# Seven block products in place of eight, in three of the eight k-tile pairs of the gate and up matmuls of a transformer block

## The chip, the cores and the metric

One Trainium2 chip, one of its cores. A core has TensorE (PE in the profile), VectorE (DVE), ScalarE (ACT), GpSimd (POOL) and SyncE (SP, which issues the transfers here). The metric is the time of one execution on the device in microseconds (us); less is better.

## The reference

One layer of an encoder on 256 tokens of width 2048, all in float32:

```
xn = rms_norm(h, norm1_g); proj = xn @ w_in               # 2048 x 5120
att = differential attention (4 heads);  u = conformer convolution (1024 channels)
h  = h + concat(att, u) @ w_out                           # 2048 x 2048
hn = rms_norm(h, norm2_g)
a  = hn @ w_gate                                          # 2048 x 5632
bu = hn @ w_up                                            # 2048 x 5632
h  = h + (silu(a) * bu) @ w_down                          # 5632 x 2048
```

The change concerns the last four lines.

## The kernel before

**The split into two parts.** Every float32 factor is written as hi + lo, both of type float32r: hi is the rounded value (ScalarE, `act.copy`), lo the rest (VectorE, a subtraction). A product is then three matmuls: activation hi by weight hi (L306), activation lo by weight hi (L307), activation hi by weight lo (L312). The activation is the stationary operand (128 x 128), the weight the moving one (128 x 512).

**Chunks and blocks.** A block is 512 columns of a weight for all 256 tokens, that is two PSUM banks (tokens in two halves of 128, index m), summed over k-tiles of 128 rows. A block's k-tiles come in chunks of two: one transfer of 512 KB into `raw` (L270), one cast into `whi` (L275), one subtraction into `wlo` (L276), and 12 matmuls: the eight with the weight's hi first, then the four with its lo.

**The order.** All queues are written out by hand; nothing is reordered. `run_chunks` walks the list of chunks; when TensorE's part of chunk t is written out, the loads and splits of chunk t+2 (AHEAD = 2) have just been written. `raw` has five buffers, `whi` and `wlo` four each (RAW_BUFS, HL_BUFS), so that the split of a chunk waits until TensorE is done with the chunk four before it. Each engine takes its instructions strictly in this order. Beside the chunks run generators, resumed in the middle and at the end of each chunk: they write the norms, the attention, the convolution and the evictions, so that what they write stands in the engines' queues between two splits.

**The feed-forward part.** There are 11 blocks of 512 hidden columns. Each is a gate block of 16 k-tiles, whose result ScalarE turns into `sil` (L713), and an up block of 16 k-tiles, whose result VectorE multiplies with it (L721); then 16 transposes in TensorE (L729) and a hi/lo split (L732, L733) give the stationary tiles `ahi`, `alo` for w_down. After six blocks, and again after the other five (FGROUPS), w_down's products of these blocks are summed and added into `h` (L746). The factor 1/rms of the second norm, `rstd2`, is applied at the eviction (L713, L721).

**PSUM.** The eight banks are two pools: `acc` (four, the sums of blocks) and `aux` (four: transposes and the rest).

Of the kernel before, what the change touches and what calls it, by code (L numbers as in the profile page):

```python
# [28 lines left out]
W = 31  # L29
# [9 lines left out]
# where the rows of the gains and biases begin, 128 values to a row  # L39
# [41 lines left out]
def tile_block(  # L81
# [9 lines left out]
    lhs = ctx.enter_context(tc.tile_pool(name="lhs", bufs=KD))  # L91
# [7 lines left out]
    # ---------------------------------------------------------------- inputs and constants  # L99
# [7 lines left out]
    # the tensor engine's clock rises while the first loads are under way  # L107
# [9 lines left out]
    # a first use of the activation table before anything waits for it  # L117
# [11 lines left out]
    cw = const.tile([P, NCT, W], F32, tag="cw", name="cw")  # L129
# [15 lines left out]
    def late_constants():  # L145
# [10 lines left out]
        # q is scaled by 1/sqrt(d) through its gain  # L156
        act.mul(gb[:, 0, :], gb[:, 0, :], 1.0 / math.sqrt(DH))
        hd = DH // 2
        for i, key in enumerate("qk"):
            for m in range(NM):  # L160
                t = const.tile([P, 2, DH], F32, tag=f"gcs{key}{m}", name=f"gcs{key}{m}")
# [12 lines left out]
    def negative_lambda():  # L174
        """-lambda = exp(l2) - exp(l1) - lambda_init"""
# [5 lines left out]
    def rsqrt_mean(dst, ss, n, eps):  # L181
        """dst = (ss / n + eps) ** -0.5 on a few columns."""
# [4 lines left out]

    def lhs_pair(pfx, k):
        hi = lhs.tile([P, S], F32R, tag="lhi", name=f"{pfx}hi{k}")
        lo = lhs.tile([P, S], F32R, tag="llo", name=f"{pfx}lo{k}")  # L190
        return hi, lo

    def split_scaled(pair, src, scale):
        """hi + lo = src * scale, src in PSUM."""
# [21 lines left out]
    # banks of the aux pool that are read in a later stage than they are written  # L216
# [7 lines left out]
    # work of the vector engine that fills what the stream leaves free  # L224
# [12 lines left out]
    def side_step():  # L237
        """One step of the two oldest chains by turns: a step waits for the one before it."""
# [11 lines left out]
    def block(w, cols, ks, xs, done=None, bkey=None, first=True, last=True, spare=False, cuts=()):  # L250
        """Products of the k-tiles ks with columns of w, summed in two banks."""
# [6 lines left out]
        while i < len(ks):  # L258
# [4 lines left out]
                               done=done if i == len(ks) else None, spare=spare))  # L263

    def split_chunk(w, k0, nk, cols, width, **_):
        view = lambda t: t.rearrange("p (k n) -> p k n", n=width)[:, :nk]
        raw = view(wp.tile([P, NK * N], F32, tag="raw", name="raw", bufs=RAW_BUFS))
        o = 0
        for c, n in cols:
            sp.dma_start(out=raw[:, :, o : o + n],  # L270
# [539 lines left out]
```

## Time and profile before

| what | value |
|---|---|
| median of three runs | 1091.2 us (1090.16 to 1091.35) |
| profiled execution: span from the first to the last instruction | 1089.8 us |
| TensorE busy | 1079.0 us (99%) |
| weight loads of TensorE | 894.0 us (82%) |
| VectorE busy | 647.1 us (59%) |
| ScalarE busy | 509.6 us (47%) |
| moved by DMA | 203 MB, mean 186 GB/s |

The page gives only the span of the profiled execution; the median of the runs lies 1.4 us above it, which is what lies around the first and last instruction. Busy time of TensorE counts overlapping matmuls as they lie, so that a busy TensorE says only that it hardly waits; how fast it goes is read from the distance between the starts of neighbouring matmuls in the timeline. A wait costs time only if TensorE takes part in it.

### The profile page before, as it was taken

The page shows a single profiled execution, that of the slowest core. Times are in us where ns is not written, and L with a number is a line of the kernel's source. Part 1 is how long each engine was busy: PE and PEld are TensorE (multiplying, and loading weights), DVE is VectorE, ACT ScalarE, POOL GpSimd, SP SyncE. Part 2 cuts the span into 40 slices and gives each one's busy share as a digit, 9 for nine tenths or more (in the row PEclk, how much of TensorE's full clock was granted, in tenths as well). Part 3 has the DMA queues.
Part 4 walks back from the last instruction along what each step waited for, and adds up shares of the span by engine and source line. Part 5 has one row for each costly group of instructions (what it writes and reads, how often), then busy time and mean ns, then how long its engine had stood idle before and what let it go on. Part 6 is the DMA issues. An engine that isn't in the chain of part 4 may idle for free.

```text
span 1089.8 us, 13224 instructions
## 1 busy us (share of the span) xinstructions
PE 1079.0 (99%) x4952; PEld 894.0 (82%) x4952; DVE 647.1 (59%) x828; ACT 509.6 (47%) x719; POOL 49.1 (5%) x77
## 2 busy tenths in 40 slices
PE   8999999999999999999999999999999999999998
PEld 7988888877888888888888888888888888888886
DVE  4799989898766544544545454444454454544443
ACT  6644566755754544434444343333443444433332
POOL 0030112210100100000000000000000000000000
PEclk9999999999999999999999999999999999999999
DMA  8756665554456557666575555556666656653654
GB/s 241 233 177 198 190 189 161 154 169 155 155 181 206 174 172 220 187 192 189 168 214 184 192 192 193 192 187 190 194 186 192 189 169 211 186 192 108 219 204 146
DMA packets 118733, 203.02 MB, mean 186 GB/s; under 512 B 6932, under 2 KB 28878, under 8 KB 118668
## 3 DMA queue, kind: packets, MB, share of 16 engines
q1 hardware_dynamic: 118608, 202.14, 59.7%
q8 instruction: 39, 0.64, 0.2%
q14 instruction: 26, 0.21, 0.1%
q10 hardware_dynamic: 60, 0.03, 0.0%
HBM read 200.04 MB, written 2.10 MB: 185 GB/s over the span
## 4 chain that ended last, share of the span: by engine, by line
PE 92%; DVE 3%; ACT 2%; POOL 1%; issue 1%; DMA 1%; SPq 1%; DVEq 0%; ACTq 0%
PE acc L307 30%; PE acc L312 30%; PE acc L306 30%; DVE y L431 1%; DVE wlo L276 1%; PE ps_a L729 1%; ACT whi L275 1%; DMA h<-in_x_dram 1%; PE ps_o L643 1%; ACT junk L355 0%; POOL rsq L185 0%; PE ps_h L686 0%; SPq L360 0%; POOL fq L186 0%; SPq L270 0%
## 5 line engine op out<-in xcount | busy, mean ns | idle before, releaser
L276 DVE TENSOR_TENSOR wlo<-raw,whi 128x1024 fp32r<-128x1024 f32 (+1 forms) x377 | 456.4, 1221 | 337.3 <-ACT whi L275 304.5
L275 ACT CAST whi<-raw 128x1024 fp32r<-128x1024 f32 (+1 forms) x377 | 390.8, 1051 | 366.4 <-PE acc L307 326.6
L306 PE MATMUL acc<-whi,hhi 128*128 128x512 f32 x704 | 274.8, 390 | 0.0
L307 PE MATMUL acc<-whi,hlo 128*128 128x512 f32 x704 | 274.1, 389 | 0.0
L312 PE MATMUL acc<-wlo,hhi 128*128 128x512 f32 x704 | 189.2, 391 | 0.0
L307 PEld LDWEIGHTS acc<-whi,hlo 128*128 128x128 f32 x704 | 132.2, 188 | 27.3
L306 PEld LDWEIGHTS acc<-whi,hhi 128*128 128x128 f32 x704 | 132.2, 188 | 27.2
L312 PEld LDWEIGHTS acc<-wlo,hhi 128*128 128x128 f32 x704 | 131.4, 188 | 26.8
L306 PE MATMUL acc<-whi,ahi 128*128 128x512 f32 x384 | 150.7, 392 | 0.0
L307 PE MATMUL acc<-whi,alo 128*128 128x512 f32 x384 | 150.5, 392 | 0.0
L306 PE MATMUL acc<-whi,xhi 128*128 128x512 f32 (+1 forms) x352 | 130.0, 376 | 2.8 <-ACT xhi L196 2.8
L307 PE MATMUL acc<-whi,xlo 128*128 128x512 f32 (+1 forms) x352 | 128.6, 372 | 0.5 <-DVE xlo L197 0.4
L431 DVE SCALAR_TENSOR_TENSOR y<-upad,cw,y 128x256 f32<-128x256 f32 x240 | 103.6, 481 | 3.5 <-ACT y L424 3.0
L312 PE MATMUL acc<-wlo,ahi 128*128 128x512 f32 x384 | 103.6, 391 | 0.0
L312 PE MATMUL acc<-wlo,xhi 128*128 128x512 f32 (+1 forms) x352 | 88.7, 377 | 1.4 <-DVE wlo L276 1.2
L306 PEld LDWEIGHTS acc<-whi,ahi 128*128 128x128 f32 x384 | 72.1, 188 | 15.9
L307 PEld LDWEIGHTS acc<-whi,alo 128*128 128x128 f32 x384 | 72.1, 188 | 15.3
L312 PEld LDWEIGHTS acc<-wlo,ahi 128*128 128x128 f32 x384 | 71.9, 188 | 15.6
L306 PEld LDWEIGHTS acc<-whi,xhi 128*128 128x128 f32 x352 | 66.5, 189 | 14.7 <-ACT xhi L196 3.2
L307 PEld LDWEIGHTS acc<-whi,xlo 128*128 128x128 f32 x352 | 66.6, 189 | 11.9 <-DVE xlo L197 0.9
L312 PEld LDWEIGHTS acc<-wlo,xhi 128*128 128x128 f32 x352 | 62.3, 190 | 13.0 <-DVE wlo L276 2.2
L733 DVE TENSOR_TENSOR alo<-ps_a,ahi 128x512 fp32r<-128x512 f32 x22 | 15.2, 691 | 46.0 <-ACT ahi L732 46.0
(138 smaller groups left out, 544.2 us busy)
## 6 DMA issues: line engine op xcount, KB each, us to landing
raw<-in_w_gate_dram SPq DMA_DIRECT2D x88, 512.0 KB, 4.4
raw<-in_w_up_dram SPq DMA_DIRECT2D x88, 512.0 KB, 4.5
raw<-in_w_down_dram SPq DMA_DIRECT2D x88, 512.0 KB, 4.2
raw<-in_w_in_dram SPq DMA_DIRECT2D x48, 512.0 KB, 3.7
raw<-in_w_out_dram SPq DMA_DIRECT2D x32, 512.0 KB, 3.7
raw<-in_w_in_dram SPq DMA_DIRECT2D x62, 256.0 KB, 3.6
h<-in_x_dram SPq DMA_DIRECT2D x6, 256.0 KB, 6.1
out_dram<-h SPq DMA_DIRECT2D x6, 256.0 KB, 2.5
```

The source lines that it names most:

```text
L275: act.copy(hi, raw)
L276: dve.tensor_tensor(lo, raw, hi.bitcast(F32), ALU.subtract)
L306: pe.matmul(ps[m], xhi[:, ms], hi[:, j, :], start=c["first"] and j == 0, stop=False)
L307: pe.matmul(ps[m], xlo[:, ms], hi[:, j, :], start=False, stop=False)
L312: pe.matmul(ps[m], xhi[:, ms], lo[:, j, :], start=False, stop=c["last"] and j == nk - 1)
L431: dve.scalar_tensor_tensor(y[:, ct, :], src, wk, y[:, ct, :], ALU.mult, ALU.add)
L643: pe.matmul(o[:, m, :], wT[:, (0 if m == 0 else 1 + k), :], v_sb[k][:, hd * E : (hd + 1) * E], start=k == 0, stop=k == m)
L729: pe.transpose(pt[:, i, m * P : (m + 1) * P], aa[m][:, c : c + P], ident)
L733: dve.tensor_tensor(lo, pt, hi.bitcast(F32), ALU.subtract)
```

## The change

Block 0 of the feed-forward part stays as it was. In blocks 1 to 10 gate and up are computed together, as one product of a 2 x 2 arrangement: the rows are the two token halves, the inner index is a pair of k-tiles (k and k+8), the columns are up and gate. For three of the eight pairs (k = 0, 1, 2; NS = 3) this 2 x 2 product is formed with seven block products by Strassen's scheme in Winograd's form, from sums and differences of the activations (made once, in `make_forms`) and of the weight tiles (made for each pair, in `round_pair`). The other ten k-tiles are multiplied as before, in five chunks for gate and five for up. The seven products are summed in seven PSUM banks (the eighth is QX) over the three pairs, and the plain chunks are summed into those banks that each output needs last (Q2, Q4 for gate; Q3, QX for up). ORDER gives the 13 units of a block: s is a pair, g and u are plain chunks. `products_done` and `block_done` combine the banks into the four outputs. `make_forms` also multiplies the activations with `rstd2`, so that the evictions of these blocks need no scale.

Beside this: `whi` and `wlo` have three buffers instead of four and `raw` four instead of five; in the new blocks the cast runs three units ahead and the subtraction two; w_down is passed three times (after 4, 4 and 3 blocks) instead of twice; the stationary tiles for w_down share the pool of those of x and h, in tiles of two; some constants move to another pool; a pass of `transposed` is spread over more resumptions.

```diff
-RAW_BUFS = 5
+RAW_BUFS = 4
-HL_BUFS = 4
+HL_BUFS = 3
-FGROUPS = (6, 5)
+FGROUPS = (4, 4, 3)
+HK = KD // 2
+NS = 3
+REST = [k for k in range(KD) if k % HK >= NS]
+TWOS = [tuple(REST[i : i + 2]) for i in range(0, len(REST), 2)]
+BY_DMA = []
+ORDER = "sgggsggusuuuu"
+Q1, Q6, Q7, Q5, Q2, Q4, Q3, QX = range(8)
+PRODUCTS = ((Q1, 0, 5), (Q6, 5, 1), (Q7, 6, 2), (Q5, 4, 3), (Q2, 1, 6), (Q4, 3, 0), (Q3, 2, 4))
+HI_AHEAD, LO_AHEAD = 3, 2
...
     def run_chunks():
-        ready = deque()
         n = len(chunks)
-        i = 0
+        i = j = 0
         for t in range(n):
-            while i < min(n, t + 1 + lead(t)):
+            hi_lead, lo_lead = lead(t)
+            while i < min(n, t + 1 + hi_lead):
                 if i in before:
                     before[i]()
-                ready.append(split_chunk(**chunks[i]))
+                chunks[i]["load"](chunks[i])
+                chunks[i]["round"](chunks[i])
                 i += 1
-            multiply(chunks[t], *ready.popleft())
+                if hi_lead == lo_lead:
+                    chunks[j]["split"](chunks[j])
+                    j += 1
+            while j < min(n, t + 1 + lo_lead):
+                chunks[j]["split"](chunks[j])
+                j += 1
+            chunks[t]["multiply"](chunks[t])
...
@@ transposed: (was the end of up_done)
-            hi = fp.tile([P, 2, S], F32R, tag="ahi", name="ahi", bufs=FGROUPS[0] * 2)
-            lo = fp.tile([P, 2, S], F32R, tag="alo", name="alo", bufs=FGROUPS[0] * 2)
+            hi, lo = lhs_two("a", j * (N // P) + 2 * t)
             act.copy(hi, pt)
+            yield
             dve.tensor_tensor(lo, pt, hi.bitcast(F32), ALU.subtract)
...
             yield
+            yield
...
+    forms = {}
+    def make_forms():
+        fp = ffn["pool"]
+        ones = fp.tile([P, P], F32, tag="sum0", name="ones")
+        pool.memset(ones, 1.0)
+        diag = fp.tile([P, S], F32, tag="sum1", name="diag")
+        for m in range(NM):
+            act.activation(diag[:, m * P : (m + 1) * P], ident, AF.Copy, scale=rstd2[m])
+        yield
+        yield
+        ps = aux_ps.tile([P, N], F32, tag="aux", name="ps_r")
+        for m in range(NM):
+            pe.matmul(ps[:, m * P : (m + 1) * P], ones, diag[:, m * P : (m + 1) * P], start=True, stop=True)
+        yield
+        rb = fp.tile([P, S], F32, tag="sum2", name="rb")
+        act.copy(rb, ps[:, :S])
+        yield
+        hn = [fp.tile([P, HK, S], F32, tag="wt", name="hn"), fp.tile([P, HK, S], F32, tag="wb", name="hn", bufs=2)]
+        for k in range(KD):
+            while k not in hT:
+                yield
+            t = hn[k // HK][:, k % HK, :]
+            hi, lo = hT[k]
+            dve.tensor_tensor(t, hi.bitcast(F32), lo.bitcast(F32), ALU.add)
+            dve.tensor_tensor(t, t, rb, ALU.mult)
+            if k % 4 == 3:
+                yield
+        a11, a21 = (hn[0][:, :NS, m * P : (m + 1) * P] for m in range(NM))
+        a12, a22 = (hn[1][:, :NS, m * P : (m + 1) * P] for m in range(NM))
+        fhi = fp.tile([P, 7, NS, P], F32R, tag="fhi", name="fhi")
+        flo = fp.tile([P, 7, NS, P], F32R, tag="flo", name="flo")
+        f = fp.tile([P, 7, NS, P], F32, tag="wh", name="sums", bufs=2)
+        dve.scalar_tensor_tensor(f[:, 4], a21, -1.0, a22, ALU.mult, ALU.subtract)
+        dve.scalar_tensor_tensor(f[:, 5], f[:, 4], -1.0, a11, ALU.mult, ALU.subtract)
+        dve.tensor_tensor(f[:, 6], a11, a21, ALU.subtract)
+        dve.tensor_tensor(f[:, 2], a12, f[:, 5], ALU.subtract)
+        act.copy(fhi[:, 0], a11)
+        act.copy(fhi[:, 1], a12)
+        act.activation(fhi[:, 3], a22, AF.Copy, scale=-1.0)
+        yield
+        for i in (4, 5, 6, 2):
+            act.copy(fhi[:, i], f[:, i])
+        for i, a in ((0, a11), (1, a12)):
+            dve.tensor_tensor(flo[:, i], a, fhi[:, i].bitcast(F32), ALU.subtract)
+        dve.scalar_tensor_tensor(flo[:, 3], a22, -1.0, fhi[:, 3].bitcast(F32), ALU.mult, ALU.subtract)
+        yield
+        for i in (4, 5, 6, 2):
+            dve.tensor_tensor(flo[:, i], f[:, i], fhi[:, i].bitcast(F32), ALU.subtract)
+        yield
+        nr = HK - NS
+        chi = fp.tile([P, 2 * nr, S], F32R, tag="chi", name="chi")
+        clo = fp.tile([P, 2 * nr, S], F32R, tag="clo", name="clo")
+        for i in range(2):
+            act.copy(chi[:, i * nr : (i + 1) * nr], hn[i][:, NS:])
+        yield
+        for i in range(2):
+            dve.tensor_tensor(clo[:, i * nr : (i + 1) * nr], hn[i][:, NS:],
+                              chi[:, i * nr : (i + 1) * nr].bitcast(F32), ALU.subtract)
+        plain = {k: (chi[:, i, :], clo[:, i, :]) for i, k in enumerate(REST)}
+        forms.update(hi=fhi, lo=flo, plain=plain)
+    def load_pair(c):
+        c["b"] = ffn["pool"].tile([P, 4, N], F32, tag="wb", name="wb", bufs=2)
+        for i, w in enumerate((w_up, w_gate)):
+            sp.dma_start(out=c["b"][:, 2 * i : 2 * i + 2, :],
+                         in_=w.rearrange("(k p) n -> p k n", p=P)[:, c["k"] :: HK, c["col"] : c["col"] + N])
+    def round_pair(c):
+        fp = ffn["pool"]
+        assert "hi" in forms
+        b = c["b"]
+        c["t"] = t = fp.tile([P, 4, N], F32, tag="wt", name="wt")
+        c["hi"] = fp.tile([P, 7, N], F32R, tag="wh", name="wh", bufs=2)
+        dve.tensor_tensor(t[:, 2:4], b[:, 1:3], b[:, 0:1].to_broadcast([P, 2, N]), ALU.subtract)
+        dve.tensor_tensor(t[:, 1], b[:, 1], t[:, 3], ALU.add)
+        dve.tensor_tensor(t[:, 0], t[:, 1], b[:, 3], ALU.subtract)
+        act.copy(c["hi"][:, 4:], b[:, 1:])
+        act.copy(c["hi"][:, :4], t)
+    def split_pair(c):
+        c["lo"] = ffn["pool"].tile([P, 7, N], F32R, tag="wl", name="wl", bufs=2)
+        dve.tensor_tensor(c["lo"][:, 4:], c["b"][:, 1:], c["hi"][:, 4:].bitcast(F32), ALU.subtract)
+        dve.tensor_tensor(c["lo"][:, :4], c["t"], c["hi"][:, :4].bitcast(F32), ALU.subtract)
+    def sum_bank(c, i):
+        sums = c["sums"]
+        if i not in sums:
+            tag, pool_ = ("acc", acc_ps) if i < 4 else ("aux", aux_ps)
+            sums[i] = pool_.tile([P, N], F32, tag=tag, name=f"q{i}")
+        return sums[i]
+    def multiply_pair(c):
+        while "hi" not in forms:
+            resume()
+        fhi, flo, p = forms["hi"], forms["lo"], c["k"]
+        for n, (q, f, w) in enumerate(PRODUCTS):
+            ps = sum_bank(c, q)
+            first, last = c["first"].get(q), c["last"].get(q)
+            pe.matmul(ps, fhi[:, f, p, :], c["hi"][:, w], start=bool(first), stop=False)
+            pe.matmul(ps, flo[:, f, p, :], c["hi"][:, w], start=False, stop=False)
+            pe.matmul(ps, fhi[:, f, p, :], c["lo"][:, w], start=False, stop=bool(last))
+            if n in (1, 3, 5):
+                resume()
+        resume()
+        if c["done"]:
+            start(c["done"](c["sums"]))
+    def multiply_two(c):
+        hi, lo = c["hi"], c["lo"]
+        qs = (Q3, QX) if c["kind"] == "u" else (Q2, Q4)
+        for i, k in enumerate(c["ks"]):
+            x1, x2 = forms["plain"][k]
+            for m, q in enumerate(qs):
+                ms = slice(m * P, (m + 1) * P)
+                ps = sum_bank(c, q)
+                pe.matmul(ps, x1[:, ms], hi[:, i, :], start=i == 0 and bool(c["first"].get(q)), stop=False)
+                pe.matmul(ps, x2[:, ms], hi[:, i, :], start=False, stop=False)
+        resume()
+        for m, q in enumerate(qs):
+            ms = slice(m * P, (m + 1) * P)
+            for i, k in enumerate(c["ks"]):
+                pe.matmul(sum_bank(c, q), forms["plain"][k][0][:, ms], lo[:, i, :], start=False,
+                          stop=i == 1 and bool(c["last"].get(q)))
+        resume()
+        if c["done"]:
+            start(c["done"](c["sums"]))
+    def fast_block(j):
+        units, sums = [], {}
+        left = dict(s=list(range(NS)), g=list(TWOS), u=list(TWOS))
+        for kind in ORDER:
+            what = left[kind].pop(0)
+            c = dict(kind=kind, sums=sums, done=None, first={}, last={})
+            if kind == "s":
+                c.update(k=what, col=j * N, load=load_pair, round=round_pair, split=split_pair,
+                         multiply=multiply_pair, uses=[q for q, _, _ in PRODUCTS])
+            else:
+                c.update(ks=what, w=w_gate if kind == "g" else w_up, nk=2, width=N, cols=[(j * N, N)],
+                         rows=slice(what[0], what[1] + 1, what[1] - what[0]), by_dma=what in BY_DMA,
+                         load=load_chunk, round=round_chunk, split=split_chunk, multiply=multiply_two,
+                         uses=(Q3, QX) if kind == "u" else (Q2, Q4))
+            units.append(c)
+        assert not any(left.values())
+        for q in range(8):
+            users = [c for c in units if q in c["uses"]]
+            users[0]["first"][q] = users[-1]["last"][q] = True
+        [c for c in units if c["kind"] == "s"][-1]["done"] = products_done
+        units[-1]["done"] = lambda sums: block_done(j, sums)
+        chunks.extend(units)
+    halfway = {}
+    def products_done(q):
+        fp = ffn["pool"]
+        w1, u2, u3, w4 = (fp.tile([P, N], F32, tag=f"sum{i}", name=f"sum{i}") for i in range(4))
+        act.copy(w1, q[Q1])
+        yield
+        yield
+        dve.tensor_tensor(u2, q[Q6], w1, ALU.add)
+        dve.tensor_tensor(u3, q[Q7], u2, ALU.add)
+        dve.tensor_tensor(w4, q[Q5], u3, ALU.add)
+        dve.tensor_tensor(u2, q[Q5], u2, ALU.add)
+        yield
+        dve.tensor_tensor(w1, q[Q2], w1, ALU.add)
+        dve.tensor_tensor(u3, q[Q4], u3, ALU.add)
+        act.activation(w1, w1, AF.Silu)
+        act.activation(u3, u3, AF.Silu)
+        halfway.update(g=(w1, u3), u=(u2, w4))
+    def block_done(j, q):
+        while "g" not in halfway:
+            yield
+        g, u = halfway.pop("g"), halfway.pop("u")
+        yield
+        for m, i in enumerate((Q3, QX)):
+            dve.tensor_tensor(u[m], q[i], u[m], ALU.add)
+        yield
+        for m in range(NM):
+            dve.tensor_tensor(u[m], u[m], g[m], ALU.mult)
+        yield
...
+            if j:
+                fast_block(j)
+                continue
             block(w_gate, j * N, range(KD), fh, silu_done)
...
-    lead = lambda t: 1 if t < len(XPARTS) else AHEAD
+    lead = lambda t: (1, 1) if t < len(XPARTS) else (HI_AHEAD, LO_AHEAD) if "kind" in chunks[t] else (AHEAD, AHEAD)
```

More of the change, by code (lines that the diff above doesn't have):

```diff
@@ L186, in rsqrt_mean, with lhs_two @@
         pool.tensor_tensor(dst, t[:, :k], neghalf[:, :k], ALU.pow)
+    halves = {}
     def lhs_pair(pfx, k):
-        hi = lhs.tile([P, S], F32R, tag="lhi", name=f"{pfx}hi{k}")
-        lo = lhs.tile([P, S], F32R, tag="llo", name=f"{pfx}lo{k}")
-        return hi, lo
+        if k % 2 == 0:
+            halves[pfx] = lhs_two(pfx, k)
+        return tuple(t[:, k % 2, :] for t in halves[pfx])
+    def lhs_two(pfx, k):
+        return tuple(lhs.tile([P, 2, S], F32R, tag=f"l{x}", name=f"{pfx}{x}{k}") for x in ("hi", "lo"))
     def split_scaled(pair, src, scale):
@@ L702, in out_done @@
             ffn["pool"] = ctx.enter_context(tc.tile_pool(name="ffn", bufs=1))
+            start(make_forms())
     ffn = {}
@@ L711, in silu_done @@
         for m in range(NM):
-            sil[m] = ffn["pool"].tile([P, N], F32, tag="sil", name="sil", bufs=4)
+            sil[m] = ffn["pool"].tile([P, N], F32, tag=f"sum{m}", name="sil")
             act.activation(sil[m], ps[m], AF.Silu, scale=rstd2[m])
@@ L723, in up_done, with transposed @@
         yield
+        yield from transposed(j, aa)
+    def transposed(j, aa):
         for t in range(N // P // 2):
```

49 lines of the change are left out of this document (30 added, 19 removed).

## The prediction

> **What bounds the kernel now.** I read the page first (engines, slices, chain), then busy time by stage, then the timeline of one block.
>
> ```profile
> span 1089.8 us, 13224 instructions
> PE 1079.0 (99%) x4952; PEld 894.0 (82%) x4952; DVE 647.1 (59%) x828; ACT 509.6 (47%) x719; POOL 49.1 (5%) x77
> DVE  4799989898766544544545454444454454544443
> PEclk9999999999999999999999999999999999999999
> PE 92%; DVE 3%; ACT 2%; POOL 1%; issue 1%; DMA 1%; SPq 1%; DVEq 0%; ACTq 0%
> ```
>
> TensorE is busy from end to end at the full granted clock, and 92% of the chain that ended last is its work. VectorE is nearly full in the first quarter (convolution) and half full in the feed-forward stage. By stage:
>
> ```profile
> core 0: us, PE busy (x) PEld busy (x) DVE busy (x) ACT busy (x) POOL busy (x), PEclk, DMA share, GB/s
> 0.00:100.00 100.00, 95.32 (x523) 83.18 (x524) 78.51 (x134) 56.20 (x91) 11.46 (x27) 0.98 0.72 214
> 400.00:500.00 100.00, 100.00 (x454) 82.83 (x453) 50.16 (x47) 42.84 (x46) 0.00 (x0) 1.00 0.61 182
> ```
>
> Between 400 and 500 us TensorE does not wait at all; VectorE and ScalarE have half their time left, DMA a third. A matmul removed there is worth its distance to the next one, as long as VectorE, which gets the new work, delivers in time. The prices, from the timeline (VectorE, then TensorE and ScalarE):
>
> ```profile
> 189.13 0.42 DVE L543 TENSOR_TENSOR t<-qn,gcsk 128x256 f32<-128x256 f32 x1
> 189.46 0.42 DVE L544 TENSOR_TENSOR t<-qn,gcsk 128x256 f32<-128x256 f32 x1
> 189.92 0.69 DVE L545 TENSOR_TENSOR t<-t,t 128x512 f32<-128x512 f32 x1
> 190.53 1.27 DVE L431 SCALAR_TENSOR_TENSOR y<-upad,cw,y 128x256 f32<-128x256 f32 x3
> 406.47 3.50 DVE L276 TENSOR_TENSOR wlo<-raw,whi 128x1024 fp32r<-128x1024 f32 x3 [0.25 <-ACT whi L275]
> 406.56 1.07 PE L312 MATMUL acc<-wlo,hhi 128*128 128x512 f32 x4
> 409.28 1.07 PE L312 MATMUL acc<-wlo,hhi 128*128 128x512 f32 x4
> 409.48 1.05 ACT L275 CAST whi<-raw 128x1024 fp32r<-128x1024 f32 x1 [1.14 <-PE acc L307]
> ```
>
> TensorE: the two L312 rows are 12 matmuls apart: 2.72 us a chunk, 0.2267 us a matmul. A pair of 21 matmuls takes 4.76 us. A buffer comes free 0.20 us after the next matmul's start (409.48 against 409.28). VectorE, start to start: 1.14 us for 1024 elements ((3.50 - 1.22) / 2), 0.33 for 256 (189.13 to 189.46), 0.61 for 512 (189.92 to 190.53); so 1.04 ns an element, 0.47 for 384, 1.41 for 1280, 1.67 for 1536, 2.20 for 2048. An operation that reads the one just before starts 0.13 later (189.46 to 189.92 is 0.46).
>
> **The matmuls removed.** Each new block has three pairs of seven products instead of eight, three matmuls a product: 183 matmuls for 192. Ten blocks: 90 x 0.2267 = **-20.4 us**. All of it lies on TensorE's path. The Trainium skill, "TensorE: Matmul & The Clock Gate", section "Back-to-back issue gap", gives about 216 ns for 512 columns; by that the saving would be an estimated 19.4 us. The rows here show 0.2267, and the measurement decides.
>
> **The activation forms (`make_forms`), once, in block 0.** VectorE gets, between units 5 and 9 of that block's 16 chunks, 16 additions and 16 dependent products of 128x256 (0.46 + 0.33 = 0.79 a k-tile, 3.16 a resumption of four), four sums of 384 (4 x 0.47 + three waits of 0.13, and 0.06 each for the two three-operand ones: 2.4), seven subtractions of 384 (3.35) and two of 1280 (2.8): 21.2 us. They stand in its queue between the splits that TensorE waits for. Walk it from the start of unit 5; a chunk takes 2.72 on TensorE and needs its lo 1.81 after its start. Split 7 ends at 1.34, the first four k-tiles at 4.5, split 8 at 5.64, eight more at 11.96, split 9 at 13.1 (due 12.69: 0.4 late). Four k-tiles and the sums bring split 10 to 19.8 (due 15.81: 4.0 late), the seven subtractions split 11 to 24.3 (due 22.5: 1.8), the last two split 12 to 28.2 (due 27.05: 1.2); split 13 is in time. TensorE loses **+7.4 us** in that stretch. If VectorE were one chunk further ahead it is 4.7; with ScalarE's 9 casts for the forms between, 10. I take the walk. Two float32 matmuls of 128 columns (rms into columns) cost **+0.2**, priced as transposes:
>
> ```profile
> 403.50 0.93 PE acc L312 x4
> 447.97 0.93 PE acc L312 x4
> 625.87 0.92 PE acc L312 x4
> 802.10 0.93 PE acc L312 x4
> ```
>
> (Chain of waits: one block lasts 447.97 - 403.50 = 44.47, 0.95 more than 192 matmuls, for 16 transposes.)
>
> **VectorE within a new block.** By these prices: three pairs, each 1.14 + 0.61 + 0.61 + 0.26 of waits + 1.67 + 2.20 = 6.5; ten chunks of 1.14; ten combinations of 0.61 with 0.4 of waits; two lo parts of 0.61: 38.7 us in a block of 183 x 0.2267 + 0.95 = 42.4. It fits, with 3.7 us to spare, but not evenly. With three `wlo` buffers the last u chunk's split waits until TensorE leaves unit 9. From there VectorE has, in its queue's order: that split (done 1.34 after unit 10's start), six combinations of `products_done` (to 5.26), the next block's first pair (9.13), two splits (11.4), two additions and two products of `block_done` (the last ends 13.9). TensorE has units 10, 11, 12 and the pair: 36 + 21 matmuls, 12.9 to 13.0; then come the transposes, which need that last product. TensorE waits some 0.8 us, behind it the whole next unit. Seven places where a new block follows a new block: **+5.6**. If VectorE is 0.8 faster over that chain it is nothing; with another 1.2 of waits, 14. I take the walk, since all its terms have rows.
>
> **Entries into new blocks after plain chunks** (block 0 to 1, and twice after w_down). Three plain chunks ahead the split and the pair's rounding come together, and ScalarE's second cast lies between:
>
> ```profile
> L275 ACT CAST whi<-raw 128x1024 fp32r<-128x1024 f32 x375 | 389.6, 1054 | 364.9 <-PE acc L307 326.6 <-DMA raw<-in_w_down_dram 30.2 <-DMA raw<-in_w_in_dram 4.1
> L275 ACT CAST whi<-raw 128x512 fp32r<-128x512 f32 x2 | 1.2, 616 | 1.5 <-DMA raw<-in_w_in_dram 1.5
> L746 DVE TENSOR_TENSOR h<-h,acc 128x512 f32<-128x512 f32 x14 | 9.0, 684 | 6.2 <-PE acc L312 6.2
> L721 DVE SCALAR_TENSOR_TENSOR a<-acc,rstd,sil 128x512 f32<-128x512 f32 x22 | 15.5, 748 | 9.6 <-PE acc L312 9.6
> ```
>
> 0.86 ns an element: 1.93 us for 2048. Counted from the chunk two before the pair (which starts at 5.44), rounding ends at 1.3, the cast at 3.3, the pair's lo at 5.5, two splits at 7.8, and only then comes the eviction of the last plain block (0.68; 0.75 in block 0). The third product, Q7, needs that bank at 6.8 and gets it at 8.5: 1.7 + 1.7 + 1.8 = **+5.2**; from 0, if another bank is free, to 7.
>
> **The pace of a matmul.** It is not the same everywhere. w_down's first pass, 576 matmuls with stationary tiles of the ffn pool, took 802.10 - 625.87 - 44.47 = 131.8 us, 0.2288 each. And in the output projection, with other tiles:
>
> ```profile
> 342.75 0.40 PE L306 MATMUL acc<-whi,mchi 128*128 128x512 f32 x1
> 343.91 0.39 PE L307 MATMUL acc<-whi,mclo 128*128 128x512 f32 x1
> ```
>
> that is 0.232. The forms lie in the ffn pool, w_down's tiles now in that of h. Nearest is w_down's pace: 1830 x 0.0021 - 1056 x 0.0021 = **+1.6**. Ends: -2.2 (all at 0.2267) and +7.5 (forms at 0.232).
>
> **What costs nothing.** The buffers that fall from 4 to 3 and 5 to 4 also serve the crowded first quarter. There TensorE waited for a lo once:
>
> ```profile
> PE acc L312 <- DVE wlo L276: 1.2, 1, 1.2
> ```
>
> VectorE is hidden behind TensorE there; where a chunk of lead is lost in each of the two crowded spells (near 187 and 223 us) it would cost 2 x 2.72 = 5.4. I take 0: VectorE hardly waits in that stretch, so it is behind the buffers, not ahead. The transfers carry the same bytes. The third pass of w_down adds eight additions of 0.68 to `h`, beside chunks in which VectorE is idle half the time; SP's loads for the pairs queue behind `raw` loads and come some ten us early.
>
> **Sum.** -20.4 + 7.4 + 0.2 + 5.6 + 5.2 + 1.6 = -0.4: a span of 1089.4. The median lies 1.4 above the span, so 1090.8 us. About 0.2% (2.2 us) is what a measurement of this kernel tells from no change.
>
> **Rivals.** *The entries hide* (32%). My waits at block borders and entries come from a queue that I walked at full prices; VectorE has 3.7 us to spare a block, and the rows show no wait of TensorE in this stage. Without both, and with the forms as walked: -20.4 + 7.4 + 0.2 + 1.6 = -11.2, 1080 us. Against it: both waits follow from the queue's order.
>
> *VectorE becomes the bound* (22%). The place is the stretch from unit 9 to the transposes of the next block. It holds 13.9 us of VectorE's work, all behind one buffer, and takes over from 13.0 on; each further 0.1 us costs 0.7 over seven places. In the rows VectorE often waits 0.25 to 0.6 for a cast. Two or three of these, 1.2 us in all, give 7 x 1.2 = 8.4: 1099 us.
>
> *The clock drops* (4%). The wait of 4.0 us in block 0 is the longest after the start; in the first 100 us, the only stage with long waits, the clock stood at 0.98. One chunk at half the clock adds 2.7: 1093.5. The same page of the Trainium skill, "Why this matters for your kernels", says a gap above about 3 us brings the lower clock back; no row after 100 us shows such a gap.
>
> *The matmuls do not go* (2%): the built program has 88 fewer TensorE instructions, 90 less the two of the forms, which speaks against it; then 1111.
>
> **How the numbers follow.** The forecast has 40%; its own range is 1085 to 1096, in which 15 points are faster than by 0.2%, 15 within and 10 slower. With the rivals: faster 0.15 + 0.32 + 0.01 = 0.48, same 0.16, slower 0.10 + 0.22 + 0.04 = 0.36. The range of 8 in 10 goes from 1078 (the entries hide and the pace stays at 0.2267) to 1100.
>
> **What would show it.** 4952 - 88 TensorE records; waits of TensorE on VectorE in block 0 near 7 us, one of 1.7 us in the first pair after plain chunks, one under 1 us before the transposes of each new block; block borders 42.4 to 44 us apart. Wrong would be a VectorE that is full over a whole block, waits of TensorE on ScalarE or DMA, or a pace of 0.23 and more in the pairs.

## The result and the profile after

The changed kernel takes 1100.7 us in the median (1099.45 to 1102.25), against 1091.3 (1090.16 to 1091.48) for the kernel before on the same chip: a ratio of 1.0086, 95% interval 1.0070 to 1.0103. It is slower by 9.4 us; the prediction was 1090.8 with 1078 to 1100. First the page of the changed kernel:

```profile
span 1100.5 us, 13218 instructions
PE 1073.3 (98%) x4866; PEld 880.1 (80%) x4866; DVE 833.3 (76%) x1051; ACT 556.0 (51%) x741; POOL 43.6 (4%) x78
DVE  4799989898765798879555788798765486987634
PEclk8999999999999989999999999999999999999999
PE 77%; DVE 13%; issue 3%; ACT 3%; DMA 2%; SPq 1%; POOL 1%; DVEq 0%; ACTq 0%; POOLq 0%
```

TensorE has 86 matmul records less, yet the span grew by 10.7 us. Its share of the chain that ended last fell from 92% to 77%, and VectorE's rose from 3% to 13%. VectorE is busy for 186 us more; single slices of the new blocks reach nine tenths. Two slices of the granted clock are an 8, the first and the fifteenth (385 to 413 us); before, all were 9. What TensorE waited for (us in total, times, longest), the whole execution:

```profile
PE acc L344 <- DVE wlo L308: 5.8, 4, 3.3
PE acc L338 <- ACT whi L299: 3.9, 2, 2.5
PE q L885 <- DVE h L979: 3.4, 2, 1.7
PE acc L338 <- ACT xhi L216: 2.5, 1, 2.5
PE q L885 <- DVE a L761: 2.4, 1, 2.4
PE ps_a L772 <- DVE sum L967: 2.2, 9, 0.3
```

Before, of these only the `xhi` row (2.8 us) and one `wlo` wait of 1.2 us were there, both in the first 350 us. All the others are new and lie behind 350 us: the forms (L308, three of the four), the entries into new blocks (L979, L761), the block borders (L967), and one that the sum did not have, `whi` on ScalarE. A wait on ScalarE was one of the prediction's own signs of being wrong. Stage by stage, from the starts of the first matmuls of each stage in the timeline (us):

| stage | before | after |
|---|---|---|
| all ahead of the feed-forward part | 353.9 | 354.05 |
| gate and up, block 0 | 44.4 (mean of a block) | 52.36 |
| gate and up, ten blocks | 443.8 | 440.97 (134.46 + 175.14 + 131.37) |
| w_down | 132.75 + 110.32 | 88.09 + 88.10 + 72.29 |

The ten new blocks together gained less than 3 us, block 0 lost 8, and w_down lost 5.4, though it has as many matmuls as before. The new blocks and the end, by stretches (PE, PEld, DVE, ACT, POOL busy, granted clock, DMA share, GB/s):

```profile
350.00:400.00 50.00, 45.40 (x194) 35.81 (x194) 40.17 (x69) 25.70 (x37) 2.63 (x5) 0.97 0.49 156
400.00:450.00 50.00, 47.57 (x206) 38.65 (x206) 39.77 (x39) 24.62 (x22) 0.00 (x0) 0.97 0.67 226
700.00:800.00 100.00, 99.17 (x439) 80.27 (x438) 81.28 (x80) 48.98 (x46) 0.00 (x0) 1.00 0.53 177
1050.00:1055.00 5.00, 3.25 (x8) 2.57 (x9) 3.07 (x3) 3.14 (x3) 0.00 (x0) 0.67 0.73 269
```

In steady new blocks (700 to 800) VectorE is at 81% and TensorE nearly full at full clock. The losses sit in block 0, at the entry behind it, and at the end, and at each of these the granted clock is below 1. The entry at 407 us and the stretch behind the wait at the end, in TensorE's timeline:

```profile
407.56 0.40 PE L887 MATMUL q<-wl,fhi 128*128 128x512 f32 x1
410.39 0.80 PE L885 MATMUL q<-wh,fhi 128*128 128x512 f32 x1 [2.43 <-DVE a L761]
410.98 0.63 PE L886 MATMUL q<-wh,flo 128*128 128x512 f32 x1
...
413.12 0.53 PE L885 MATMUL q<-wh,fhi 128*128 128x512 f32 x1
413.48 0.39 PE L886 MATMUL q<-wh,flo 128*128 128x512 f32 x1
...
1051.75 0.80 PE L338 MATMUL acc<-whi,ahi 128*128 128x512 f32 x1 [2.49 <-ACT whi L299]
1052.35 0.63 PE L339 MATMUL acc<-whi,alo 128*128 128x512 f32 x1
```

Behind both waits the next seven and eight matmuls start late, most of them 0.43 us apart in place of 0.23: half the clock, which costs 1.5 and 1.7 us. A third such spell, 1.9 us, lies behind the wait of 3.30 us in block 0. A block border, where the idle that the row names (0.16 and 0.27) is less than what is lost:

```profile
458.00 0.39 PE L887 MATMUL q<-wl,fhi 128*128 128x512 f32 x1
458.55 0.33 PE L772 MATMUL ps_a<-ident,sum 128*128 128x128 f32 x1 [0.16 <-DVE sum L967]
459.15 0.55 PE L772 MATMUL ps_a<-ident,sum 128*128 128x128 f32 x3 [0.27 <-DVE sum L967]
459.45 0.48 PE L902 MATMUL q<-whi,chi 128*128 128x512 f32 x1
```

From the last matmul of the pair to the first behind four transposes is 1.45 us. The same step without a wait, in the kernel before, takes 0.59:

```profile
402.67 0.40 PE L307 MATMUL acc<-whi,hlo 128*128 128x512 f32 x1
403.26 1.18 PE L312 MATMUL acc<-wlo,hhi 128*128 128x512 f32 x4
```

So this border costs 0.86, and the seven cost 0.83 to 0.87 each. (A block has eight transposes, in two groups of four, in both kernels: 88 rows for 11 blocks, not 16 a block.)

And the end. The chain that ended last, in order of time (start, us, what), through w_down's last pass:

```profile
1039.97 0.24 PE acc L339
1040.24 1.06 ACT whi L299
1041.32 1.23 DVE wlo L308
1042.55 0.61 DVE h L979
1043.17 0.36 SPq L981
...
1044.34 6.22 DMA raw<-in_w_down_dram
...
1050.66 1.05 ACT whi L299
```

SP issues the stores of `out` (L981) and the loads of `raw` (L294) from one queue, in order. The store waits for the addition into `h`; that addition stands on VectorE behind a split (L308), which stands behind a cast, which waits for a `whi` buffer that TensorE frees. Only then do the next loads go out, and they take 6.2 us to arrive. The kernel before has the same queue; its casts also waited for the loads, but with four and five buffers there was enough split ahead that TensorE never noticed:

```profile
1031.12 0.95 SPq L748 DMA_DIRECT2D out_dram<-h  x2
1032.17 12.77 SPq L270 DMA_DIRECT2D raw<-in_w_down_dram  x10
```

```profile
1036.26 1.05 ACT L275 CAST whi<-raw 128x1024 fp32r<-128x1024 f32 x1 [8.00 <-DMA raw<-in_w_down_dram]
```

### The profile page after: what moved, and what is told of

Its sections match the earlier page's. It is cut to its first block, busy times and chain, and to the rows that moved or that the text cites. A ratio compares the mean times of both kernels' runs of the same rounds, so it can differ in the third digit from the quotient of the medians.

```text
span 1100.5 us, 13218 instructions
## 1 busy us (share of the span) xinstructions
PE 1073.3 (98%) x4866; PEld 880.1 (80%) x4866; DVE 833.3 (76%) x1051; ACT 556.0 (51%) x741; POOL 43.6 (4%) x78
## 4 chain that ended last, share of the span: by engine, by line
PE 77%; DVE 13%; issue 3%; ACT 3%; DMA 2%; SPq 1%; POOL 1%; DVEq 0%; ACTq 0%; POOLq 0%
PE acc L338 15%; PE acc L339 15%; PE acc L344 15%; PE q L902 7%; PE q L903 7%; PE q L908 6%; DVE wlo L308 4%; PE q L885 3%; PE q L887 3%; PE q L886 3%; ACT whi L299 2%; DMA raw<-in_w_down_dram 1%; DVE wl L868 1%; PE ps_a L772 1%; DVE sum L964 1%
## 5 line engine op out<-in xcount | busy, mean ns | idle before, releaser
L308 DVE TENSOR_TENSOR wlo<-raw,whi 128x1024 fp32r<-128x1024 f32 (+1 forms) x317 | 384.2, 1220 | 222.5 <-ACT whi L299 215.3
L902 PE MATMUL q<-whi,chi 128*128 128x512 f32 x400 | 157.6, 394 | 0.0
L903 PE MATMUL q<-whi,clo 128*128 128x512 f32 x400 | 156.6, 391 | 0.0
L908 PE MATMUL q<-wlo,chi 128*128 128x512 f32 x400 | 108.6, 393 | 0.0
L885 PE MATMUL q<-wh,fhi 128*128 128x512 f32 x210 | 83.4, 397 | 5.8 <-DVE h L979 3.4
L903 PEld LDWEIGHTS q<-whi,clo 128*128 128x128 f32 x400 | 75.1, 188 | 16.4
L902 PEld LDWEIGHTS q<-whi,chi 128*128 128x128 f32 x400 | 75.1, 188 | 16.1
L908 PEld LDWEIGHTS q<-wlo,chi 128*128 128x128 f32 x400 | 74.6, 188 | 16.2
L887 PE MATMUL q<-wl,fhi 128*128 128x512 f32 x210 | 83.1, 396 | 0.0
L886 PE MATMUL q<-wh,flo 128*128 128x512 f32 x210 | 82.4, 392 | 0.0
```

What stands on the lines that cost most here:

```text
L308: dve.tensor_tensor(c["lo"], c["raw"], c["hi"].bitcast(F32), ALU.subtract)
L885: pe.matmul(ps, fhi[:, f, p, :], c["hi"][:, w], start=bool(first), stop=False)
L886: pe.matmul(ps, flo[:, f, p, :], c["hi"][:, w], start=False, stop=False)
L887: pe.matmul(ps, fhi[:, f, p, :], c["lo"][:, w], start=False, stop=bool(last))
L902: pe.matmul(ps, x1[:, ms], hi[:, i, :], start=i == 0 and bool(c["first"].get(q)), stop=False)
L903: pe.matmul(ps, x2[:, ms], hi[:, i, :], start=False, stop=False)
```

## The experiments

Theory: the matmuls bring their 20.4 us, and four separate losses outweigh it: the forms in block 0, the entries, the borders, and the end (stores in SP's queue with fewer buffers behind them). Rival: one loss in several places, a VectorE that is short of time, so that a wait removed in one place comes back in another.

**The end: stores on another queue.**

```diff
-                    sp.dma_start(out=out[m * P : (m + 1) * P, hs], in_=h[m][:, hs])
+                    act.dma_start(out=out[m * P : (m + 1) * P, hs], in_=h[m][:, hs])
```

> The changed kernel with the stores of the output issued by ScalarE's queue instead of SP's; nothing else. Theory A (the loads at the end are late because they stand in SP's queue behind a store, which waits for the addition into h, which now stands on VectorE behind a split that waits for a buffer): the waits of 2.5, 1.4 and 0.2 us in w_down's last pass go, with them the half clock after the first: 6 us less than the changed kernel's 1100.7, near 1094.7 (ratio to before 1.003). Rival (four raw buffers are too few for the memory's pace at the end, whoever issues the stores): the waits stay, 1100 to 1101 (1.009).

1094.7 us, ratio 1.0037 (1.0023 to 1.0052). The last pass took 65.88 us in place of 72.29. SP's queue, in one row, issues loads only and without a pause for a store:

```profile
1019.65 50.95 SPq L294 DMA_DIRECT2D raw<-in_w_down_dram  x20
```

The last pass holds no wait of TensorE, and between 1050 and 1055 us the clock is back at 1.00 (it was 0.67). The end is confirmed, with the half clock that belonged to it.

**The end: the buffers alone, in the kernel before.**

```diff
-RAW_BUFS = 5
+RAW_BUFS = 4
-HL_BUFS = 4
+HL_BUFS = 3
```

> The kernel before with four raw buffers and three hi and lo buffers, nothing else of the change. Theory A: the first quarter loses nothing, but at the three block borders of w_down's last pass TensorE waits for late loads: 1 to 5 us slower than before, 1092.5 to 1096. Rival 1 (the short last pass of three blocks is the cause, not the buffers): no change, 1091.3. Rival 2 (the crowded first quarter needs the buffers): slower by 2 to 5 us, with waits before 350 us.

1093.9 us, ratio 1.0026 (1.0015 to 1.0036). From the feed-forward part to the last pass the stages keep their lengths within 0.1. All ahead of it took 352.2 us in place of 353.9, and the difference lies in the first 28 us, where the kernel before had a spell of half the clock in its profiled execution and this one had none. The last pass goes from 110.32 to 113.90. TensorE's waits from 350 us on are one row, where the kernel before has none:

```profile
PE acc L306 <- ACT whi L275: 2.7, 2, 1.5
```

So the smaller buffers cost nothing up to the last pass and 3.6 us in it, without any of Strassen's work.

**The end: the third pass alone, in the kernel before.**

```diff
-FGROUPS = (6, 5)
+FGROUPS = (4, 4, 3)
```

> The kernel before with w_down passed after 4, 4 and 3 blocks (FGROUPS) and nothing else. Theory (the end is lost by the buffers and SP's queue): a third pass alone costs nothing, 1091.3 +- 1. Rival: the shorter last pass or the additional eight additions into h cost by themselves, 1 to 4 us: 1092.5 to 1095.

1091.3 us, ratio 0.9997 (0.9988 to 1.0006). The third pass is free, as the prediction had it.

**Block 0: the forms without their 16 additions.** This kernel leaves out the lo part of the activations.

```diff
-            dve.tensor_tensor(t, hi.bitcast(F32), lo.bitcast(F32), ALU.add)
-            dve.tensor_tensor(t, t, rb, ALU.mult)
+            dve.tensor_tensor(t, hi.bitcast(F32), rb, ALU.mult)
```

> The changed kernel, whose forms leave out the addition of the activations' lo part (16 additions of 128x256 on VectorE less; the forms are made of hi alone). Theory (VectorE's burst in block 0 delays the splits; the wait above 2.4 us halves the clock after it): waits of TensorE in block 0 fall from 5.1 us to below 1 and the matmuls stay at 0.23 us there: 6.5 to 7 us less than the changed kernel, near 1094 (1.0025). Rival (block 0 waits for ScalarE's casts of the forms or for their order, not for VectorE's amount): below 2 us less, 1099.

1094.4 us, ratio 1.0029 (1.0018 to 1.0040). Block 0 fell from 52.36 to 45.32 us and TensorE has no wait between 350 and 400 us. Sixteen additions, each with a dependent product behind it, some 7.4 us of VectorE's queue, were worth 7.0 us of block 0: 5.1 us of waits and 1.9 of half clock behind the longest.

**Entries: another order of banks.**

```diff
-Q1, Q6, Q7, Q5, Q2, Q4, Q3, QX = range(8)
+Q1, Q6, Q2, Q4, Q7, Q5, Q3, QX = range(8)
```

> The changed kernel with the sums Q7 and Q5 in banks of the aux pool and Q2 and Q4 in the acc pool (numbers of the banks exchanged, order of the products unchanged). Theory (after plain chunks Q7 waits for a bank that VectorE evicts late, and the longest of these waits halves the clock): the waits of 2.4, 1.7 and 1.7 us fall to below 0.5 each, since Q2 asks for the bank 1.4 us later, and the half clock near 410 us goes: 5 to 7 us less than the changed kernel, 1094 to 1096. Rival (the wait only moves to Q2 and lasts as long): below 2 us less, 1099 to 1100.

1097.0 us, ratio 1.0056 (1.0041 to 1.0071). The three waits fall from 2.43, 1.70 and 1.70 to 1.04, 0.34 and 0.34:

```profile
PE q L885 <- DVE a L761: 1.0, 1, 1.0
PE q L885 <- DVE h L979: 0.7, 2, 0.3
```

The three stages of new blocks became shorter by 2.76, 1.35 and 1.30, 5.4 us together, as expected. About 1.4 of the first 2.76 is the half clock behind the wait: with the stores on ScalarE, where the wait is as long as ever but no half clock follows, that stage took 133.08. The median gained only 3.7; in the profiled execution the last pass took 74.1 us, 1.8 more than in the changed kernel, with two spells of half clock. The mechanism holds; the end, still unmended here, took a part back.

**Borders: transposes half a chunk later.**

```diff
             for m in range(NM):
                 dve.tensor_tensor(u[m], u[m], g[m], ALU.mult)
             yield
+            yield
             yield from transposed(j, u)
```

> The changed kernel with one more resumption in block_done, between the last two products and the transposes of a block, so that TensorE's transposes stand half a chunk later in its queue. Theory (the border loss): TensorE waits at each new block for the last product of VectorE, 0.86 us each as start-to-start distances show, seven times where a new block follows a new block; half a chunk later VectorE is done, and 5 to 6 us go: 1094 to 1096. Rival 1: what waits is only moved, since the banks and the buffers behind the transposes come later too, and TensorE waits as long at the next product: 1100 to 1101. Rival 2: the 0.86 us are the price of 16 transposes, not a wait: 1100.5.

1103.0 us, ratio 1.0097 (1.0082 to 1.0111). My theory fell; the first rival, that the wait only moves, was right. (The median lies 2.3 us above the changed kernel's, but the two intervals overlap.) The four blocks in a row took 174.88 us in place of 175.14. The wait for `sum` is gone, and there is one for `alo` instead (TensorE, then ScalarE):

```profile
504.41 1.08 PE L908 MATMUL q<-wlo,chi 128*128 128x512 f32 x4
505.99 0.66 PE L772 MATMUL ps_a<-ident,sum 128*128 128x128 f32 x4 [0.49 <-DVE alo L776]
```

```profile
502.82 1.91 ACT L864 CAST wh<-wt 128x2048 fp32r<-128x2048 f32 x1 [6.28 <-DVE wt L862]
504.63 0.57 ACT L774 CAST ahi<-ps_a 128x512 fp32r<-128x512 f32 x1
```

The second group of transposes needs the bank that the first group's `ahi` and `alo` still read, and that cast stands on ScalarE behind the 1.91 us cast of the next pair.

**Borders: half a chunk more between the groups of transposes too.**

```diff
             for i in range(2):
                 actT[j * (N // P) + 2 * t + i] = (hi[:, i, :], lo[:, i, :])
             yield
             yield
+            yield
```

> The changed kernel with two edits at the block borders: the transposes half a chunk later, as in the run before, and one more resumption between two groups of four transposes in `transposed`. Late transposes alone moved the wait: TensorE then waited 0.5 us, seven times, for `alo`, because the second group of transposes needs the bank that the first group's split still reads, and ScalarE's cast of a pair (1.91 us) stands ahead of that split. Theory: with half a chunk more between the groups this wait goes too, each border gets back its 0.86 us, and the changed kernel's time falls by 5 to 6 us to 1095 to 1096. Rival: VectorE and ScalarE are late by an amount that follows the transposes wherever they are put; the wait appears again, at the third or fourth group or at the next block's first pair, and the time stays at 1100 to 1103.

1098.2 us (1094.48 to 1102.07), ratio 1.0064 (1.0044 to 1.0084). No wait for `sum` is left, and of those for `alo` only one of 0.2 us, in w_down's last pass. The stage of four blocks took 173.59 us, that is 0.52 less at each of its three borders, and the stage of three 130.42, 0.48 less at each of its two. So 0.5 of the 0.86 was to be had; in the second pair of a block 0.15 to 0.2 us are now lost ahead of a product with `wl`. The total fell less than the 5 to 6 expected, and its runs differ by 7 us; the last pass of the profiled one, at 73.6 us with a half-clock spell, is no better than in the changed kernel.

**Three edits together: stores, banks, late transposes.**

> The changed kernel with three of the single edits together: output stores issued by ScalarE, the order of the banks that lets the first pair after plain chunks begin without the two banks still to be evicted, and the transposes half a chunk later. If the losses are separate, as my theory says, they add: 1100.7 - 6.2 (end) - 5.4 (entries) - 5.5 (borders) = 1083.6, and with less half clock perhaps 1082; faster than the kernel before by 0.7%. If they are one loss in different places (VectorE is short of time and each wait removed comes back elsewhere), 1092 or more.

1089.2 us, ratio 0.9977 (0.9967 to 0.9987): faster than the kernel before. The border term did not come, as its own run shows; with 6.0 for the stores and 5.4 for the banks the sum is 1100.7 - 6.0 - 5.4 = 1089.3. By stages, the new blocks are 6.1 us shorter than in the changed kernel and the last pass 5.7 (66.62). So the other two add, and the rival of one loss in many places does not hold for them.

**Four edits: with the spread transposes.**

> The kernel with three edits (stores on ScalarE, order of the banks, late transposes; 1089.2 us) and the additional resumption between groups of transposes. Its trace shows 3.4 us of waits for `alo` at the seven borders, by start-to-start distances 0.6 to 0.86 us each. Theory: they go, 4.2 to 6 us: 1083.5 to 1085. Rival (the wait moves again): 1089.

1086.3 us, ratio 0.9954 (0.9939 to 0.9969). Against three edits, the three stages of new blocks fell by 0.80, 1.25 and 0.81: 2.9 us in all, 0.41 a border: less than the 4.2 to 6 expected, but most of the wait did not move again.

**The forms' additions on GpSimd.**

```diff
+        for k in range(KD):
...
+            pool.tensor_tensor(hn[k // HK][:, k % HK, :], hi.bitcast(F32), lo.bitcast(F32), ALU.add)
...
-            dve.tensor_tensor(t, hi.bitcast(F32), lo.bitcast(F32), ALU.add)
             dve.tensor_tensor(t, t, rb, ALU.mult)
-            if k % 4 == 3:
+            if k % 2:
                 yield
```

> The kernel of the run before (four edits) with the 16 additions hi + lo of make_forms moved from VectorE to GpSimd, written four resumptions ahead of the products, and the products spread two k-tiles to a resumption instead of four. Nothing is left out. Theory (block 0 is lost to VectorE's queue): VectorE has 16 x 0.46 = 7.4 us less between units 5 and 12, TensorE's waits for wlo in block 0 go as they did when the additions were left out (-6.8 us): 1077 to 1078. Rival: GpSimd is slow at 256 elements (its 128-element products took 0.58 to 0.64 us each) or slows VectorE, and the products wait for it: 0 to +5 us against the run before.

1087.2 us, ratio 0.9962 (0.9947 to 0.9977): no gain, as the rival had it. GpSimd's 16 additions, and VectorE beside them:

```profile
365.61 17.10 POOL L799 TENSOR_TENSOR hn<-hhi,hlo 128x256 f32<-128x256 f32 x16
```

```profile
371.53 1.76 DVE L308 TENSOR_TENSOR wlo<-raw,whi 128x1024 fp32r<-128x1024 f32 x1
373.21 3.65 DVE L811 TENSOR_TENSOR hn<-hn,rb 128x256 f32<-128x256 f32 x4
...
383.71 1.42 DVE L811 TENSOR_TENSOR hn<-hn,rb 128x256 f32<-128x256 f32 x4
385.05 1.21 DVE L308 TENSOR_TENSOR wlo<-raw,whi 128x1024 fp32r<-128x1024 f32 x1
```

While GpSimd adds, a split takes 1.76 us, and behind it 1.21; four products take 3.65, and behind it 1.42. The Trainium skill, "SBUF — State Buffer", section "SBUF: two separate sides", says that these two engines share one pair of ports, taken for a whole instruction when VectorE has two inputs in SBUF. These rows agree as far as they go: VectorE is slower as long as GpSimd adds. Block 0 still gained 2.8 us (49.55), but the first stage of new blocks lost 4.6 (135.24 against 130.68): the first pair came late (TensorE waited 0.97 and 1.60 us for `wl`), and behind that 12 matmuls went at half the clock. The products had also been spread over more resumptions, so how much of the delay is GpSimd's and how much the spreading's is not separated.

**The forms in fewer, larger, independent operations.**

```diff
-        for k in range(KD):
+        for k in range(0, KD, 4):
...
+            for i, t in zip((k, k + 2), ts):
+                hi, lo = halves["h", i]
+                dve.tensor_tensor(t, hi.bitcast(F32), lo.bitcast(F32), ALU.add)
+            for t in ts:
+                dve.tensor_tensor(t, t, rb.to_broadcast([P, 2, S]), ALU.mult)
+            yield
```

> The kernel with four edits (1086.3 us), with the additions and products of make_forms done for two k-tiles at once (128x512 in place of 128x256) and so written that no operation reads the one just before it: two additions, then two products to a resumption. All work stays on VectorE. By the measured spacings a resumption costs 4 x 0.61 = 2.44 us in place of 3.16, four times: 2.9 us less in VectorE's queue. Theory (block 0 is lost to VectorE's queue, one for one): the wait of 3.3 us at the third of the four stretches falls below 1, block 0 goes from 52.34 to about 49.5, and the slow matmuls behind that wait go too: 1083 to 1084. Rival (the work is only moved, and the first pair is late instead, as when GpSimd made the additions): 1086 to 1087.

1083.0 us (1082.77 to 1083.08), ratio 0.9924 (0.9908 to 0.9941). Block 0 took 49.18 us. On VectorE the four k-tiles of a resumption:

```profile
373.11 1.29 DVE L810 TENSOR_TENSOR hn<-hhi,hlo 128x512 f32<-128x512 f32 x2
374.32 1.29 DVE L812 TENSOR_TENSOR hn<-hn,rb 128x512 f32<-128x512 f32 x2
375.52 1.29 DVE L810 TENSOR_TENSOR hn<-hhi,hlo 128x512 f32<-128x512 f32 x2
```

2.41 us (373.11 to 375.52) in place of 3.18 in the changed kernel (374.88 to 378.06), four times, and block 0 is 3.2 us shorter than with four edits (52.34): here it pays for VectorE's queue one for one. The longest wait in block 0 is 0.97, no matmuls at half the clock follow, and the clock between 350 and 450 us is 1.00. This version does the whole computation and beats both kernels.

## Why the prediction was wrong, step by step

**The matmuls removed** (-20.4) came. So did the balance as such: several losses of a few us each, together of the size of the gain. What failed first is a term that the sum put at nothing; a rival at 4% and smaller errors of size did the rest.

**"What costs nothing" failed, and is the largest miss.** I looked at the smaller buffers in the crowded first quarter, and there they do cost nothing (353.9 against 354.05, and the run with small buffers). I wrote of the third pass and the loads as covered, but did not walk SP's queue through the last pass, where stores stand between loads. The price is 6.4 us (72.29 against 65.88 with the stores elsewhere): 3.6 of it is the buffers alone (the run of the kernel before with small buffers), about 1.7 the half clock behind the wait; the rest, about 1, I did not separate. The trace of before had the row to see it by: a cast that waited 8.00 us for its load, covered only by what was split ahead.

**The clock rival was the second miss.** I gave it 4% and one place, 2.7 us. It came three times in the profiled execution, 5 us in all (counted in the end, the entries and block 0), and twice behind waits of 2.43 and 2.49 us, shorter than the 4.0 that I feared. How often it comes differs between executions of the same kernel: the mean granted clock of the four is 0.992 to 0.995, their times 1102.25 to 1099.45, so that it was partly luck on which side of 1100 one fell.

**The forms** were forecast at +7.6 with the two matmuls and measured +8.0, but not from the same parts: the waits are 0.52, 3.30 and 0.78 us, 5.1 by start-to-start distances, where the walk had 7.4; the half clock filled the difference. That VectorE's queue is the cause is shown by the run without the lo part and the one with larger operations.

**The entries** were forecast at +5.2 and measured 6.3 (2.6, 1.85, 1.85 from start to start) and 1.5 of half clock. The mechanism, a bank that the last plain block has still to give up, is shown by the order of banks.

**The borders** were forecast at 0.8 each, +5.6, and measured 0.83 to 0.87, +5.9. The reason given, VectorE's last product, was only a part of it: with that out of the way another wait stands there, on a bank and on ScalarE, and a border still costs 0.7. With both out of the way 0.5 came back.

**The pace** was forecast at +1.6 and is about +2.2: the new blocks go at 0.2291 us a matmul (+4.4), nearer to the far end than I took, and w_down's passes at 0.2267 (-2.2), the other end. Why a stationary tile in one place is slower than in another was not tried.

Added up, -20.4 + 8.0 + 7.8 + 5.9 + 2.2 + 6.4 = +9.9, where the span grew by 10.7. The step from span to time, 1.4 in the prediction, is 1.75 in the profiled execution (1102.25 and 1100.5). **VectorE as the bound**, the rival of 22%, gave the nearest time (1099) for a reason that did not occur: VectorE's 13.9 us at the borders cost what was forecast, and no more.

## What to carry to other kernels

An algorithm that removes 2% of the matmuls is worth nothing by itself when its preparation sits in front of a busy engine: each place where it starts, ends or changes the order pays its own wait, and these must be walked one by one, to the very end of the kernel. Before a buffer is taken away, look in the trace for the longest idle time of *any* engine that the buffers now hide, and walk the in-order queue behind it; a store in a queue of loads is the first suspect. When a wait is removed, name what is late next, and by how much, before counting the gain.

## What the runs showed of the hardware

**Half the clock behind short waits.** In the changed kernel, waits of 2.43 and 2.49 us were followed by seven and eight late matmuls. The wait at the entry has the same place and length in four other kernels (with the stores on ScalarE, the shortened forms, the late and the spread transposes), and behind none of them did the granted clock fall. With the stores on ScalarE:

```profile
406.58 0.42 PE L887 MATMUL q<-wl,fhi 128*128 128x512 f32 x1
409.44 0.50 PE L885 MATMUL q<-wh,fhi 128*128 128x512 f32 x1 [2.44 <-DVE a L761]
```

What differs is where the wait lies in time. Between 25 us and the last matmuls, every spell of half the clock in the 13 traces lasts 3.41 us or twice that, and within an execution the spells start whole multiples of 3.41 us apart (at 389.50, 409.98 and 1051.68 in the changed kernel). Intervals of this grid around the entry, in the changed kernel and then with the stores on ScalarE (columns as in the stretches above):

```profile
406.57:409.98 3.41, 1.39 (x7) 0.78 (x5) 3.41 (x4) 1.35 (x2) 0.00 (x0) 1.00 0.68 226
409.98:413.39 3.41, 3.00 (x7) 2.42 (x8) 1.01 (x2) 0.00 (x0) 0.00 (x0) 0.50 0.85 271
```

```profile
404.47:407.88 3.41, 2.54 (x11) 1.72 (x10) 3.41 (x3) 2.51 (x3) 0.00 (x0) 1.00 0.87 330
407.88:411.30 3.42, 1.85 (x8) 1.53 (x9) 2.17 (x3) 0.00 (x0) 0.00 (x0) 1.00 0.68 210
```

In the changed kernel most of the wait, 2.0 us, fell into one interval, in which TensorE is shown busy for 1.39 us, and the next went at half the clock. In the other kernel the same wait lay across two, busy for 2.54 and 1.85 us, and the clock stayed. In the 13 traces each of the 15 falls from full to half the clock came behind an interval with at most 1.54 us busy, and none behind one with 1.63 or more. So by these traces the idle time within one interval decides, not the length of a wait: of two waits of 0.97 and 1.60 us that ended 2.6 us apart, the first and some 0.9 us of the second fell into one (the forms on GpSimd; 1.54 us busy), and behind the single waits of 1.70 us the clock never fell. This was read from the traces afterwards; no run was made to test it. The Trainium skill, "TensorE: Matmul & The Clock Gate", section "What's actually happening", gives a free-running window of about 3.4 us that must pass idle before the clock halves; a wait of 2.4 us cannot fill it. The traces agree with the length of the window, but here a window less than half busy was enough, and the measurement decides.

**VectorE is slower beside GpSimd**: 1.76 against 1.21 us for a split, 0.91 against 0.36 for a product of 256 elements, as shown above.

**A wait is longer than the idle time beside it**: 0.43 us of idle rows at a border, 0.86 from start to start. A matmul is shown 0.39 us long where the next one starts after 0.23, so its last part hides a part of the wait. What a wait costs is read from starts.
